# Down product of a SwiGLU layer as seven block products instead of eight, with the sums of activations formed in the gate/up stage

## The chip, the core and the metric

One core of one Trainium2 chip. Its engines run at the same time, each in its own order: TensorE (PE) multiplies a 128x128 block that it has loaded with up to 512 columns, VectorE (DVE) does elementwise work, ScalarE (ACT) copies, squares and activations, GpSimd (POOL) issues some transfers and a power, SyncE (SP) issues most transfers. SBUF is the memory that engines work in, PSUM holds matmul results in 8 banks of 128x512 floats. The metric is device time in microseconds (us) of one execution, lower is better.

## What is computed

A two-layer encoder trunk over 256 + 512 rows of width 1024 (here 768 rows, six tiles of 128). Each layer runs a token mixer and then a SwiGLU, with RMSNorm before and after each. The part that matters is the second:

```python
def swiglu(h, w_gate_up, w_down):          # w_gate_up 1024 x 5632, w_down 2816 x 1024
    g, u = jnp.split(h @ w_gate_up, 2, axis=-1)
    return (jax.nn.silu(g) * u) @ w_down

x = x + rms_norm(swiglu(rms_norm(x, g_pre), ...), g_post)
```

All arrays are float32. The kernel keeps that accuracy by splitting every operand in two fp32r numbers, hi (a rounded copy, made by ACT) and lo (the rest, made by DVE), and by three matmuls for each product: hi·hi, hi·lo, lo·hi.

## The kernel before

**Feed.** `raw_src` lists every weight load in program order and `units` every pair of hi and lo that is made of one, 128x1024 floats at a time. `prepare` makes units up to a ring of five (`RING`, tags `whi`, `wlo`): a unit can be split once TensorE has used the unit five before it. `take` hands units to a product, `free` makes the next ones. Raw weights land in two buffers (`wraw`); `fetch` issues a load on SP as soon as one is free. A planner of the tile library places all instructions in each engine's queue, and every engine, SP too, then runs its queue strictly in order.

**Gate and up** (`ffn`, 22 chunks of 128 hidden units). The activations stand in `h_hi`, `h_lo`; each chunk is already done by seven block products, p1 to p7, of 12 matmuls of 384 columns, over two halves of the hidden width and two halves of the rows (tiles 0 to 2 and 3 to 5). Product p6 puts its result in bank Y (`py`), DVE reads it (`u2`, line 925), and p7 goes on adding into the same bank: between them stands only p2, 12 matmuls. At a chunk's end p3 multiplies by the gate, and POOL stores 384 KB of the chunk's 768 columns to DRAM (`act`, line 953) from a buffer `st`.

**Down** (lines 1007 to 1078). For each half `n2` of the 1024 output columns, 22 chunks are loaded again from DRAM as `araw` (SP, line 1096, two buffers), split to `ahi`, `alo`, and multiplied with the weight units (`down`): a chunk gives 6 tiles x 3 matmuls `pd` of 512 columns, 792 a layer. `Acts.prepare` runs up to six chunks ahead; the first two are loaded before the stage begins, into buffers of the pools `x` and `y` (the second one's `alo` stands in an `x` buffer), since the stage's own pool opens only when the gate/up buffers are gone. `project_end` squares and scales each finished half row; `staged` and `finish` do norms, add the residual `x` (loaded by `load_x` from DRAM into the two `x` buffers), and turn the rows for the next stage.

## Time and profile before

| | |
|---|---|
| runs, us | 1744.67, 1743.99, 1740.69 (median 1743.99) |
| profiled execution, us | 1740.31, of which the span from first to last instruction is 1738.5 |
| mean granted TensorE clock | 0.997 of full speed |
| busy share of the span | PE 98%, DVE 67%, ACT 49%, POOL 5% |
| bytes moved | 187.14 MB, 108 GB/s over the span |

The two gate/up stages lie at about 299 to 629 and 1219 to 1549 us, the down stages at 629 to 813 and 1549 to 1730. A row's `[n <-X]` or `idle before <-X` is the time for which its engine stood still just before it, and what ended that. PE rows overlap: a matmul's row is longer than the distance to the next.

### The profile page before, as it was taken

The numbers are of one execution on the slowest core, as the hardware profiler recorded it, in microseconds if no ns is written. First come the engines' busy times: TensorE is split into PE (matmuls) and PEld (weight loads), VectorE is DVE, ScalarE is ACT, GpSimd is POOL, SyncE is SP. The second block draws the span as 40 slices with busy tenths as digits, with TensorE's granted clock in tenths as the row PEclk, the third lists the DMA queues.
The fourth block names the chain that finished last, engine by engine and source line by source line (L and its number), as shares of the span: only waits on it lengthen the run. The fifth ranks groups of instructions, "written<-read, shape, count | busy, mean of one in ns | idle before, by whom it ended". The sixth has DMA issues, their size and how long they took to land. (4 is left out here: it accounts for less than half of the span.)

```text
span 1738.5 us, 25699 instructions
## 1 busy us (share of the span) xinstructions
PE 1704.5 (98%) x9714; PEld 1552.1 (89%) x9714; DVE 1172.6 (67%) x2368; ACT 854.7 (49%) x1971; POOL 82.3 (5%) x126
## 2 busy tenths in 40 slices
PE   7999999999999999999999999999899999999998
PEld 7888877999999988888999999877899999988886
DVE  7788767887777744446767777757887777744443
ACT  6777766443333333434666666756533333334432
POOL 1000001000000000001000000501000000000000
PEclk9999999999999999999999999999999999999999
DMA  5111105433331266455211111114432322256454
GB/s 206 37 38 46 38 13 196 147 129 99 100 100 64 100 204 197 152 163 179 73 38 37 37 46 39 43 43 162 151 134 100 100 100 76 88 194 197 142 158 139
DMA packets 55484, 187.14 MB, mean 108 GB/s; under 512 B 6720, under 2 KB 7104, under 8 KB 55360
## 3 DMA queue, kind: packets, MB, share of 16 engines
q1 hardware_dynamic: 51696, 167.93, 30.2%
q0 software_dynamic: 3520, 17.30, 2.5%
q8 instruction: 76, 1.25, 0.3%
q14 instruction: 48, 0.39, 0.1%
q10 hardware_dynamic: 144, 0.26, 0.0%
HBM read 155.59 MB, written 29.88 MB: 107 GB/s over the span
## 5 line engine op out<-in xcount | busy, mean ns | idle before, releaser
L202 DVE TENSOR_TENSOR wlo<-wraw,whi 128x1024 fp32r<-128x1024 f32 (+1 forms) x206 | 239.3, 1166 | 118.7 <-ACT whi L201 116.3
L201 ACT CAST whi<-wraw 128x1024 fp32r<-128x1024 f32 (+1 forms) x206 | 204.8, 1001 | 168.6 <-PE px L267 84.4
L266 PE MATMUL pd<-whi,ahi 128*128 128x512 f32 (+1 forms) x550 | 210.7, 383 | 3.8 <-ACT ahi L254 3.8
L267 PE MATMUL pd<-wlo,ahi 128*128 128x512 f32 (+1 forms) x550 | 210.3, 382 | 0.0
L268 PE MATMUL pd<-whi,alo 128*128 128x512 f32 (+1 forms) x550 | 209.1, 381 | 0.0
L255 DVE TENSOR_TENSOR alo<-araw,ahi 128x768 fp32r<-128x768 f32 x88 | 84.0, 958 | 157.5 <-ACT ahi L254 157.4
L254 ACT CAST ahi<-araw 128x768 fp32r<-128x768 f32 x88 | 73.5, 835 | 172.4 <-PE pd L267 94.6
L266 PE MATMUL pqb<-whi,hhi 128*128 128x384 f32 x384 | 136.5, 356 | 0.0
L267 PE MATMUL pqb<-wlo,hhi 128*128 128x384 f32 x384 | 128.9, 336 | 0.0
L268 PE MATMUL pqb<-whi,hlo 128*128 128x384 f32 x384 | 128.8, 335 | 0.0
L266 PEld LDWEIGHTS pd<-whi,ahi 128*128 128x128 f32 x550 | 103.9, 189 | 24.7 <-ACT ahi L254 4.7
L268 PEld LDWEIGHTS pd<-whi,alo 128*128 128x128 f32 x550 | 103.8, 189 | 20.2
L267 PEld LDWEIGHTS pd<-wlo,ahi 128*128 128x128 f32 x550 | 103.7, 189 | 19.5
L266 PE MATMUL px<-hhi,whi 128*128 128x384 f32 x352 | 117.9, 336 | 2.8 <-ACT hhi L254 2.8
L267 PE MATMUL px<-hlo,whi 128*128 128x384 f32 x352 | 117.8, 335 | 2.1 <-DVE hlo L255 2.1
L268 PE MATMUL px<-hhi,wlo 128*128 128x384 f32 x352 | 117.6, 334 | 0.0
L945 ACT ACTIVATE u<-u 128x384 f32<-128x384 f32 x44 | 23.1, 525 | 161.8 <-DVE u L944 161.8
L266 PE MATMUL po<-whi,hhi 128*128 128x512 f32 x192 | 78.0, 406 | 0.2 <-ACT hhi L254 0.2
L268 PE MATMUL po<-whi,hlo 128*128 128x512 f32 x192 | 75.4, 393 | 0.2 <-DVE hlo L255 0.2
L267 PE MATMUL po<-wlo,hhi 128*128 128x512 f32 x192 | 75.3, 392 | 0.0
L266 PEld LDWEIGHTS pqb<-whi,hhi 128*128 128x128 f32 x384 | 72.3, 188 | 1.9 <-issue 1.7
L266 PE MATMUL pqa<-whi,hhi 128*128 128x384 f32 x192 | 73.7, 384 | 0.0
(244 smaller groups left out, 4405.1 us busy)
## 6 DMA issues: line engine op xcount, KB each, us to landing
araw<-act SPq DMA_DIRECT2D x88, 384.0 KB, 3.3
wraw<-in_wgu SPq DMA_DIRECT2D x62, 512.0 KB, 3.5
wraw<-in_wd SPq DMA_DIRECT2D x44, 512.0 KB, 4.1
y_wraw<-in_wgu SPq DMA_DIRECT2D x34, 512.0 KB, 3.5
act<-st POOLq DMA_DIRECT2D x44, 384.0 KB, 2.6
wraw<-in_wb SPq DMA_DIRECT2D x32, 384.0 KB, 3.2
xd<-x SPq DMA_DIRECT2D x18, 512.0 KB, 3.1
x<-xd SPq DMA_DIRECT2D x18, 512.0 KB, 4.1
```

The costliest lines, as they stand in the source:

```text
L201: state["raw_hi"] = nc.scalar.copy(out=hi, in_=src)
L202: state["raw_lo"] = nc.vector.tensor_tensor(out=lo, in0=src, in1=hi.bitcast(F32), op=ALU.subtract)
L254: state["hi"] = nc.scalar.copy(out=hi, in_=src)
L255: state["lo"] = nc.vector.tensor_tensor(out=lo, in0=src, in1=hi.bitcast(F32), op=ALU.subtract)
L266: nc.tensor.matmul(out, ah, bh, start=start and i == 0, stop=False, skip_group_check=more)
L267: nc.tensor.matmul(out, ah, bl, start=False, stop=False, skip_group_check=more)
L268: nc.tensor.matmul(out, al, bh, start=False, stop=stop and i == last, skip_group_check=more)
L945: nc.scalar.activation(out=u, in_=u, func=AF.Silu)
```

## The change

Rows of activations A (two halves of the hidden chunks, two halves of the rows) and the down weights B are cut in 2x2 blocks, and the product is formed by the Winograd form of Strassen's scheme: seven block products, eighteen sums. A half of the hidden width is now every second chunk, so a pair of chunks (2i, 2i+1) holds both halves.

- The sums of activations (`s1` to `s4`, four DVE instructions of 128x384) are made in p3 of every odd chunk, in a buffer `st` of seven parts, and POOL stores all seven (1344 KB a pair). `u2` and `u3` have one buffer instead of two.
- Down runs seven products one after the other, each over 11 pairs in six groups (five of two pairs and one of one). A group is one load of 384 KB of activations, one weight unit and 2 x 3 tiles x 3 matmuls of 512 columns. Products are added up in PSUM where they can be (`V`, `W`); `keep` copies and `add` adds banks into `y`.
- The sums of weights (`t1` to `t4`) are made by DVE in `prepare`, from quarters that are held in the stage's pool (tags `tt`, `rb`) or loaded again into the two `wraw` buffers (t2, b22, t3).
- From the third on, split activations use the slots of `h_hi` and `h_lo`. The finish of tiles 0 to 2 stands inside the sixth product, tiles 3 to 5 end the stage.

```diff
+DOWN = ("b11", "t1", "t2", "b22", "t3", "t4")
+NGRP = (NPAIR + 1) // 2
+RAW = {"w": 2, "y": 2, "tt": 2, "rb": 2}
...
-        for n2 in range(2):
-            for i in range(NPAIR):
-                plain(wd[layer, n2, i], 1024)
+        for kind, quarter, home in (
+                ("plain", (1, 0), "w"), ("b11", (0, 0), "tt"), ("t1", (0, 1), "rb"), ("t2", (1, 1), "w"),
+                ("b22", (1, 1), "w"), ("t3", (1, 0), "w"), ("t4", None, None)):
+            for g in range(NGRP):
...
-            if upto is None and state[home] >= RAW[home]:
+            if upto is None and (state[home] >= RAW[home] or home in quarters and dpool[0] is None):
...
+                if kind in ("t1", "t2"):
+                    nc.vector.tensor_tensor(out=tt, in0=raw, in1=tt, op=ALU.subtract)
+                src = {"b11": raw, "b22": raw, "t3": rb}.get(kind, tt)
...
                 two_parts(hi[:, :n], lo[:, :n], src[:, :n])
+            if kind == "b22":
+                nc.vector.tensor_tensor(out=rb, in0=rb, in1=raw, op=ALU.subtract)
+            elif kind == "t3":
+                nc.vector.tensor_tensor(out=tt, in0=raw, in1=tt, op=ALU.subtract)
...
-            nc.vector.tensor_tensor(out=v[:, :HALF], in0=u, in1=ga.pop(c), op=ALU.mult)
-            nc.gpsimd.dma_start(out=at_hand[c], in_=v)
+            nc.vector.tensor_tensor(out=v[:, 1 - c % 2], in0=u, in1=ga.pop(c), op=ALU.mult)
+            if c % 2:
+                a12, a11, s1, s2, s4, s3, a22 = (v[:, i] for i in range(7))
+                nc.vector.tensor_tensor(out=s1, in0=s3, in1=a22, op=ALU.add)
+                nc.vector.tensor_tensor(out=s2, in0=s1, in1=a11, op=ALU.subtract)
+                nc.vector.tensor_tensor(out=s3, in0=s3, in1=a11, op=ALU.subtract)
+                nc.vector.tensor_tensor(out=s4, in0=a12, in1=s2, op=ALU.subtract)
+                nc.gpsimd.dma_start(out=at_hand[c // 4][:, :, c // 2 % 2], in_=out.pop(c // 2))
...
-                    for c in (2 * i, 2 * i + 1):
-                        for t in range(NT):
-                            down(n2, t, [c], {c: blocks[c % 2]}, c == 0, 0, final and n2 and t == NT - 1)
-                        acts.used(n2, c)
+            def run(p, gs, wk, tiles, into, first=None, last=None, w=512, part=0, more=True):
+                gs = list(gs)
+                todo = [(g, j) for g in gs for j in range(min(2, NPAIR - 2 * g))]
+                for n, (g, j) in enumerate(todo):
+                    a = acts.of(p, g)
+                    b = tuple(v[:, j * 512 + part:j * 512 + part + w] for v in wk[g])
+                    for i in tiles:
+                        products(
+                            into[i][:, :w], [(tuple(v[:, j, i * P:(i + 1) * P] for v in a), b)],
...
+            def begin(t):
+                x_of[t] = load_x(sub, t)
...
+            def add(t, c, b):
+                nc.vector.tensor_tensor(out=y[t][:, c], in0=b, in1=y[t][:, c], op=ALU.add)
+
+            def keep(t, c, b):
+                nc.scalar.copy(out=y[t][:, c], in_=b)
...
+            def one(p, g, into, first=False, last=False):
+                wk = {g: take(1)[0]}
+                run(p, [g], wk, range(3), into, first, last)
+                acts.used(1)
+                free(0)
...
+            whole(0, X, {})
+            V = banks("pv")
+            whole(1, V, {0: [do(keep, i, left, X[i]) for i in range(3)]})
+            X = None
+            W = banks("pw2_")
+            whole(2, W, {i: [do(add, i, left, V[i]), do(half_end, i, left, y[i][:, left], False)] for i in range(3)})
+            whole(3, V, {0: [do(keep, 3 + i, right, W[i]) for i in range(3)]})
+            whole(4, W, {0: [do(keep, i, right, V[i]) for i in range(3)]})
...
+            events = {
+                0: [do(add, i, right, W[i]) for i in range(3)] + [second(0), do(begin, 0), do(stage, 0, 0)],
...
+            for i in range(3):
+                run(5, gs, wk, [i], V, False, True)
+                with tc.high_priority():
+                    add(3 + i, right, V[i])
...
+                    s = self.slot(q)
+                    self.user[s] = q
+                    half, at = divmod(s, 4)
+                    hi, lo = (h[half][:, 2 * at:2 * at + n] for h in (h_hi, h_lo))
```

**SP's queue where the first layer's down stage begins.** `x_0` and `x_1` are the residual rows, `araw` the activations, `act` their DRAM copy, `tt` and `wraw` weights. Before, the two loads of activations stand ahead of `x_1`:

```order
L347 DMA x_0_8243<-xd_0_115 128x1024
L1096 DMA araw_2_7180<-act_2_4249 128x768
L1096 DMA araw_3_7186<-act_3_4250 128x768
L347 DMA x_1_8269<-xd_1_116 128x1024
L196 DMA wraw_7238<-in_wd 128x1024
L1096 DMA araw_4_7192<-act_4_4251 128x768
```

After:

```order
L389 DMA x_0_8056<-xd_0_115 128x1024
L210 DMA wraw_7492<-in_wd 128x1024
L389 DMA x_1_8097<-xd_1_116 128x1024
L1260 DMA araw_2_7181<-act_2_4249 128x768
L1260 DMA araw_3_7185<-act_3_4250 128x768
L210 DMA tt_7205<-in_wd 128x1024
L210 DMA tt_7207<-in_wd 128x1024
L1260 DMA araw_4_7189<-act_4_4251 128x768
```

The load of `x_1` has moved ahead of the third and fourth loads of activations. Its buffer is the one that holds the second activations' `alo`, in both kernels. The second layer has the same order.

**DVE's queue at the end of an odd chunk of gate/up.** `u`, `st`, `py`, `pw`, `ga`, `sv` belong to the chunks, `wraw`, `b`, `wlo` to the weights of later ones. Before, from the silu's factor to the next chunk's read of bank Y:

```order
L946 TENSOR_TENSOR st_13_6081<-st_13_6081,u_13_6062 128x384
L951 TENSOR_TENSOR u_13_6026<-pw_13_6068,u_13_6026 128x384
L202 TENSOR_TENSOR b_6101<-y_wraw_5921,b_6101 128x512
L952 TENSOR_TENSOR st_13_6081<-u_13_6026,ga_13_6040 128x384
L225 TENSOR_TENSOR y_wraw_5921<-y_wraw_5921,wraw_5919 128x512
L226 TENSOR_TENSOR wraw_5919<-y_wraw_5921,wraw_5919 128x512
L202 TENSOR_TENSOR wlo_6100<-y_wraw_5921,whi_6099 128x1024
L925 TENSOR_TENSOR u_14_6153<-py_14_6140,sv_14_6138 128x384
```

After:

```order
L994 TENSOR_TENSOR st_12_5950<-st_12_5950,u_13_6057 128x384
L1003 TENSOR_TENSOR st_12_5950<-st_12_5950 128x384
L999 TENSOR_TENSOR u_13_6021<-pw_13_6063,u_13_6021 128x384
L1004 TENSOR_TENSOR st_12_5950<-st_12_5950 128x384
L216 TENSOR_TENSOR b_6095<-y_wraw_5917,b_6095 128x512
L1000 TENSOR_TENSOR st_12_5950<-u_13_6021,ga_13_6035 128x384
L253 TENSOR_TENSOR y_wraw_5917<-y_wraw_5917,wraw_5915 128x512
L1005 TENSOR_TENSOR st_12_5950<-st_12_5950 128x384
L254 TENSOR_TENSOR wraw_5915<-y_wraw_5917,wraw_5915 128x512
L1006 TENSOR_TENSOR st_12_5950<-st_12_5950 128x384
L216 TENSOR_TENSOR wlo_6094<-y_wraw_5917,whi_6093 128x1024
L968 TENSOR_TENSOR u_14_6151<-py_14_6138,sv_14_6136 128x384
```

The four sums (lines 1003 to 1006) all stand ahead of the read of bank Y (line 968, before 925).

**DVE's queue in the down stage around the end of a set of banks.** Before, at the end of the first half of the columns:

```order
L202 TENSOR_TENSOR wlo_7667<-wraw_7562,whi_7666 128x1024
L510 TENSOR_TENSOR yf_0_7150<-pd_0_0_0_7156,gpost_6883 128x512
L510 TENSOR_TENSOR yf_1_7151<-pd_0_1_0_7160,gpost_6883 128x512
L510 TENSOR_TENSOR yf_2_7152<-pd_0_2_0_7164,gpost_6883 128x512
L510 TENSOR_TENSOR yf_3_7153<-pd_0_3_0_7168,gpost_6883 128x512
```

After, at the end of the fifth product (bank `pw_0_0`):

```order
L264 TENSOR_TENSOR tt_7205<-wraw_7859,tt_7205 128x1024
L264 TENSOR_TENSOR tt_7207<-wraw_7888,tt_7207 128x1024
L216 TENSOR_TENSOR wlo_7916<-rb_7321,whi_7915 128x1024
L264 TENSOR_TENSOR tt_7235<-wraw_7920,tt_7235 128x1024
L216 TENSOR_TENSOR wlo_7941<-rb_7323,whi_7940 128x1024
L264 TENSOR_TENSOR tt_7263<-wraw_7945,tt_7263 128x1024
L264 TENSOR_TENSOR tt_7291<-wraw_7970,tt_7291 128x1024
L216 TENSOR_TENSOR wlo_7966<-rb_7401,whi_7965 128x1024
L264 TENSOR_TENSOR tt_7319<-wraw_7999,tt_7319 128x512
L297 TENSOR_TENSOR hlo_114<-araw_32_7990,hhi_112 128x768
L1106 TENSOR_TENSOR yf_0_7154<-pw_0_0_7512,yf_0_7154 128x512
```

The six sums of the last weights (line 264), each of which reads a newly loaded `wraw`, stand ahead of the first `add` of that bank (line 1106).

## Rows read from the trace of the kernel before

**Rows 1.** The page, busy time: share of the span and instructions.

```profile
PE 1704.5 (98%) x9714; PEld 1552.1 (89%) x9714; DVE 1172.6 (67%) x2368; ACT 854.7 (49%) x1971; POOL 82.3 (5%) x126
```

**Rows 2.** Busy time by stretch: gate/up, then down; x counts instructions.

```profile
470.00:620.00 150.00, 150.00 (x867) 150.00 (x867) 105.57 (x152) 52.98 (x72) 5.96 (x11) 1.00 0.29 99
...
640.00:700.00 60.00, 60.00 (x267) 49.64 (x266) 26.94 (x27) 21.95 (x26) 0.00 (x0) 1.00 0.62 190
```

**Rows 3.** Waits over the span: total us, times, longest us.

```profile
PE pd L266 <- ACT ahi L254: 3.8, 2, 1.9
...
SPq L347 <- PE pd L268: 10.9, 2, 5.4
```

**Rows 4.** Timeline where down begins (PE's first pd at 628.77): SP, ACT, PE.

```profile
630.88 0.83 SPq L1096 DMA_DIRECT2D araw<-act  x2
637.17 0.32 SPq L347 DMA_DIRECT2D x<-xd  x1
...
639.39 0.83 ACT L254 CAST ahi<-araw 128x768 fp32r<-128x768 f32 x1 [0.40 <-DMA araw<-act]
...
639.04 0.50 PE L266 MATMUL pd<-whi,ahi 128*128 128x512 f32 x1 [1.91 <-ACT ahi L254]
```

**Rows 5.** Transfers: KB each, median us to landing; then landing of all araw.

```profile
araw<-act SPq DMA_DIRECT2D x88, 384.0 KB, 3.3
...
wraw<-in_wd SPq DMA_DIRECT2D x44, 512.0 KB, 4.1
...
DMA to landing us min/median/max: 2.8/3.3/8.1
```

**Rows 6.** Stretches after a stall: PE, PEld, DVE, ACT, POOL, granted clock, DMA share, GB/s.

```profile
636.00:640.00 4.00, 2.09 (x10) 1.42 (x9) 1.71 (x2) 2.39 (x3) 0.00 (x0) 1.00 0.85 298
...
1554.00:1558.00 4.00, 2.24 (x6) 1.82 (x7) 2.96 (x3) 2.54 (x3) 0.00 (x0) 0.76 0.74 193
...
1558.00:1562.00 4.00, 4.00 (x16) 3.20 (x15) 0.00 (x0) 0.00 (x0) 0.00 (x0) 0.82 0.82 290
```

**Rows 7.** Groups of one shape: busy us, mean ns of one, idle before.

```profile
L202 DVE TENSOR_TENSOR wlo<-wraw,whi 128x1024 fp32r<-128x1024 f32 x158 | 194.2, 1230 | 110.9 <-ACT whi L201 109.1 <-PE po L268 1.5
L201 ACT CAST whi<-wraw 128x1024 fp32r<-128x1024 f32 x158 | 165.3, 1050 | 153.0 <-PE px L267 84.4 <-PE pd L268 19.2 <-ACT ga L920 16.7
...
L255 DVE TENSOR_TENSOR alo<-araw,ahi 128x768 fp32r<-128x768 f32 x88 | 84.0, 958 | 157.5 <-ACT ahi L254 157.4
...
L254 ACT CAST ahi<-araw 128x768 fp32r<-128x768 f32 x88 | 73.5, 835 | 172.4 <-PE pd L267 94.6 <-DMA araw<-act 73.8 <-DVE wlo L202 2.6
...
L952 DVE TENSOR_TENSOR st<-u,ga 128x384 f32<-128x384 f32 x44 | 24.3, 551 | 0.1
```

**Rows 8.** Timeline of gate/up, DVE then PE: a middle chunk, then chunk 19's end.

```profile
512.49 0.56 DVE L951 TENSOR_TENSOR u<-pw,u 128x384 f32<-128x384 f32 x1 [0.37 <-PE pw L268]
...
513.75 0.55 DVE L952 TENSOR_TENSOR st<-u,ga 128x384 f32<-128x384 f32 x1
514.22 0.69 DVE L225 TENSOR_TENSOR y_wraw<-y_wraw,wraw 128x512 f32<-128x512 f32 x1
...
516.09 1.23 DVE L202 TENSOR_TENSOR wlo<-y_wraw,whi 128x1024 fp32r<-128x1024 f32 x1 [0.45 <-ACT whi L201]
517.23 0.55 DVE L925 TENSOR_TENSOR u<-py,sv 128x384 f32<-128x384 f32 x1
...
518.53 0.33 PE L266 MATMUL py<-hhi,whi 128*128 128x384 f32 x1
...
590.13 0.55 DVE L925 TENSOR_TENSOR u<-py,sv 128x384 f32<-128x384 f32 x1
...
591.33 0.33 PE L266 MATMUL py<-hhi,whi 128*128 128x384 f32 x1
```

**Rows 9.** Timeline of the end: PE's last matmul, DVE's last work.

```profile
1729.94 0.28 PE L268 MATMUL pd<-whi,alo 128*128 128x256 f32 x1
...
1733.77 1.41 DVE L445 SCALAR_TENSOR_TENSOR x<-yf,rstd_last,x 128x512 f32<-128x512 f32 x2 [2.58 <-DMA x<-xd]
```

More of the change, by code (lines that the diff above doesn't have):

```diff
@@ L891, in ffn @@
         sub = 2 * layer + 1
-        at_hand = [dram.tile([P, NT * P], F32, name=f"act{layer}_{c}") for c in range(NCH)]
+        at_hand = [
+            dram.tile([P, 7, min(2, NPAIR - 2 * g), HALF], F32, name=f"act{layer}_{g}") for g in range(NGRP)]
         a_ops = {
@@ new lines, in one, with whole @@
+            def one(p, g, into, first=False, last=False):
[3 more added lines that the diff above has]
+                free(0)
+            def whole(p, into, events):
+                for g in range(NGRP):
+                    one(p, g, into, p in (0, 1, 2) and g == 0, g == NGRP - 1)
+                    for e in events.get(g, ()):
+                        e()
+            do = lambda f, *a: lambda: f(*a)
+            X = banks("px2_")
@@ new lines, in ffn, with last_product @@
+            free(2)
+            V2 = [bank(f"pv2_{k}") for k in range(2)] if final else []
+            def last_product(i, gs, wk, first=False, last=False, parts=(0, 1)):
+                if final and i == 2:
+                    for k in parts:
+                        run(6, gs, wk, [i], {i: V2[k]}, first, last, 256, 256 * k, False)
+                else:
+                    run(6, gs, wk, [i], V, False, last)
+            for i in range(3):
+                last_product(i, gs, wk, True)
+                if i == 0:
+                    stage(2, 2)
+                    begin(3)
+                half_end(3 + i, right, y[3 + i][:, right], False)
@@ new lines, in ffn @@
+            if final:
+                keep(5, left, V[2])
+            acts.used(2)
+            free(0)
+            wk = {2: take(1)[0]}
+            for i in range(3):
+                last_product(i, [2], wk)
+            acts.used(1)
+            free(0)
+            stage(2, 3)
+            begin(4)
+            gs = range(3, NGRP)
+            wk = dict(zip(gs, take(3)))
+            for g in gs:
+                acts.of(6, g)
+            free(3)
+            last_product(0, gs, wk, last=True)
@@ L1082, in trunk @@
+            last_tile(sub, 5, y[5], sq[5], x_of[5], rstd(ss4[:, 1:2], ss[:, 0:1], "last"))
     class Acts:
```

246 lines of the change are left out of this document (152 added, 94 removed).

## The prediction

> **What bounds the kernel now.** I read the busy shares first [rows 1]: TensorE is busy for 98% of the span, DVE for 67%. Then the stretches [rows 2]: 60.00 of 60 us in a down stretch, 150.00 of 150 in gate/up, both at clock 1.00, so in both stages the time is TensorE's work and whatever takes work from it is worth its full time, as long as the others keep up. DVE has room: 105.57 of 150 us in gate/up, 26.94 of 60 in down. Then the waits [rows 3], to see where TensorE stands still already: for `ahi` twice, 3.8 us, once a layer where down begins [rows 4]. The same list shows SP standing at one load until a `pd` matmul is done (10.9 us, twice); the change moves things behind that load.
>
> **What it removes.** A down stage has 22 chunks x 6 tiles x 2 halves x 3 = 792 matmuls. Afterwards it has 7 products x 11 pairs x 3 tiles x 3 = 693 of the same shape: 99 fewer. In the down stretch 267 pass in 60 us [rows 2], 0.2247 us each. 99 x 0.2247 = 22.25 us a layer, **44.5 us** in both, all on the path.
>
> **Where down begins.** Now: `pd` begins at 628.77, two chunks last until 628.77 + 36 x 0.2247 = 636.86, the load of `x_1` goes out at 637.17, when the second chunk's `alo` is used up and its buffer free. The third and fourth activations were asked for at 630.88, ahead of it, and TensorE goes on at 639.04 after 1.91 us [rows 4]. (The cast of the fourth waited for its landing until 639.39.) Afterwards the queue has `x_1` first, and the first two groups last the same 8.09 us, so the third activations are asked for at about 637.6: `x_1` at 637.17, 0.32 to issue, a little between. From there to landing it takes 2.8 us at least, 3.3 in the median, 8.1 at most [rows 5]; 512 KB of `x_1` lie just ahead, and the store of the last pair, 1344 KB in place of 384, goes out some 5 us into the stage and is still under way. The 8.1 was measured at this very place, with a 384 KB store in flight. I take 6.5: landing 644.1, cast 0.83 [rows 7], TensorE on at 644.95, and the third matmul waits some 0.5 us more for `alo`. That is 5.9 + 0.5 = 6.4 us later than 639.04, **12.8 us** for both layers; with 2.8 and 8.1 it is 2.7 and 8.0 a layer.
>
> How the store and the loads share the engines no row tells. The Trainium skill (DMA: Bandwidth & Descriptors, section "Queues, rings and completion order") says that each transfer engine takes turns between queues, packet by packet. By that the 896 KB of `x_1` and the activations run at about half of the 298 GB/s of rows 6 while the store lasts, an estimate of 6.0 us beside the 6.5; wholly behind the store it would be near 8, and the sum 3 us worse.
>
> **The clock.** After the second layer's wait, as long as the first's, the granted clock is 0.76 and 0.82 over two stretches of 4 us: (0.24 + 0.18) x 4 = 1.7 us lost. After the first layer's it stays 1.00 [rows 6]. A wait of 8 us should cost it in both; the second layer pays already: **1.7 us**. Between 0 and another 1.7 for each further stall of 2 us or more.
>
> **Four sums in each odd chunk of gate/up.** One lasts 0.55 us [rows 7], and 0.47 lie between two starts (513.75 and 514.22 [rows 8]): 1.88 us for the four. By the total DVE has the time: 5 pairs in 150 us bring 11, 105.57 becomes 117. But all four stand ahead of the read of bank Y, and p7 adds to that bank. In a middle chunk the read starts at 517.23 and ends at 517.78, p7 begins at 518.53: cover 0.75. Ahead of it DVE stands still for 0.37 (for p3's matmul) and 0.45 (for a cast that itself waits for line 225) [rows 8]. The first takes up most of one sum; the second at most its 0.45, as line 225 is put off as well. 1.88 - 0.37 - 0.45 = 1.06, less the cover 0.75: 0.3 us a pair, for some seven of the eleven. In the last chunks the cover is 591.33 - 590.68 = 0.65 [rows 8], and their loads share with the larger stores: 0.7 each for three. The first four chunks, where DVE is fuller, get 0.7 as well. 7 x 0.3 + 4 x 0.7 = 4.9; as some of it falls into waits that are there already, I take 3.5 a layer, **7 us**. Bounds: 1 (idle time takes all but the last chunks' share) and 8 (no idle time is used and the loads are late: 11 pairs x 0.75).
>
> **Feeding seven products.** A product lasts 99 x 0.2247 = 22.25 us. DVE then has 5.5 weight splits of 1.23, 5.5 activation splits of 0.96 and, for four products, 5.5 sums of the size of a split: 6.8 + 5.3 + 6.8 = 18.9 us [rows 7], 85%. In the products that also empty banks, six more of some 0.7 (the 0.69 of a 512-wide one [rows 8]) make 23.1, over the 22.25. ACT has 5.5 x (1.05 + 0.83) = 10.3 and the bank copies: hidden. The cover for DVE's overrun is the ring: with one unit a group of 4.04 us, a unit may be split four groups, 16 us, before its use. An overrun of 1 us in two products is lost in that. What is not covered by the ring is the `add` that frees a bank: six sums stand ahead of it, each after a new landing in one of two buffers. Per pair of loads 4.1 (landing [rows 5]) + 1.23 + waits, about 6, in the 8.09 us of two groups: it keeps up. I take **2 us** for both layers, from 0 to 8.
>
> At the end, an `add` more in the chain is hidden in the 2.58 us for which the last step waits for `x` [rows 9], whose load stands behind the same store as before: 0, from -1 to 1. Bank copies on ACT, 22 stores in place of 44 on POOL, the finishing of three tiles inside the sixth product: work on engines with room, 0; uncovered they are in the 8 above.
>
> **Sum.** -44.5 + 12.8 + 1.7 + 7 + 2 = -21.0 us. Against the profiled execution: 1740.3 - 21.0 = 1719.3. That execution is 3.7 below the median of the three runs; carried to the median, 1744.0 - 21.0 = **1723 us**.
>
> **Rivals.**
> (a) The covers hold: the late load lands in the median's 3.3 us (3.2 a layer in place of 6.4), gate/up pays 1 a layer. -44.5 + 6.4 + 1.7 + 2 = -34.4: **1710**. For it: most activations land in 2.8 to 3.6. Against: rows 4 and 5, 8.1 at this place.
> (b) DVE falls behind in the middle products and pays at the `add`s: they come 5 us late at the sixth product or at its successor, and the clock dips once more a layer. -21.0 + 2 x (5 + 1.7) = -7.6: **1736**. For it: 85 to 104% of DVE, and each sum waits for ACT or a landing, in order. Against: the ring's 16 us.
> (c) Slower: the reload of weights becomes the bound. t2, b22 and t3 read each weight quarter anew through two buffers; the next load goes out only when the sum has freed one. A pair of loads has 8.09 us; with landing L it takes L + 1.05 + 1.23 and some 0.2, so it decides from L = 5.6. Loads of activations and weights together then ask for 5.5 x 896 KB in 22.25 us, 226 GB/s, where 190 keeps the transfer engines at 0.62 [rows 2]: 0.74. If L goes to the 8.1 of rows 5, a pair takes 10.6, 2.5 too long, 3 pairs x 3 products x 2 layers = 45 us: 1723 + 45 = **1768**.
> (d) It doesn't do what it says. The order has the 693, so only the other terms could hide it: the same as (b).
>
> **How the numbers follow.** Chances: forecast 0.55 (own range 1715 to 1731), (a) 0.15, (b) 0.17, (c) 0.13. The range reaches from (a)'s time to some 6 us beyond (b)'s, 1709 to 1742, and leaves out (c) and a little of (a). 0.2% of the median, about what a measurement of this kernel can tell from no change, is 3.5 us: faster means below 1740.5. The forecast, (a) and most of (b) lie there, 0.81; 0.06 of (b) and of mild forms of (c) lie within; slower is 0.13.
>
> **What would show it.** Right: `pd`'s successors count 693 a layer at 0.2247; the third activations' cast ends TensorE's wait some 16 us after the stage begins; SP's wait for a matmul grows shorter in name but holds both `araw` loads; `py` waits for line 968 in tenths of a us after each odd chunk. Wrong: waits of TensorE for `wlo` in products 3 to 5 (then (c)), or for an `add` or `y_pd` of 3 us and more (then (b)); a first wait below 4 us (then (a)).

## The result, and the profile after

The changed kernel takes 1720.92 us in the median of 4 runs (1719.56 to 1724.5), the kernel before 1743.37 beside it; the ratio is 0.9876, with a 95% interval of 0.9857 to 0.9896. That is 22.4 us less; forecast were 21. The profiled execution has a span of 1718.3 us, against 1738.5.

The page's busy shares, to set beside [rows 1]:

```profile
PE 1666.2 (97%) x9483; PEld 1515.1 (88%) x9483; DVE 1298.3 (76%) x2560; ACT 887.9 (52%) x2026; POOL 83.8 (5%) x104
```

TensorE has 231 instructions less: 198 matmuls of 512 columns, and half of the 66 that the last tile's split into pieces had added (the kernel before has 132 of 256 columns, this one 66). It is busy for 38.3 us less, but the span is only 20.2 shorter, so some 18 us of new standing still lie between. DVE has 126 us more of work, the sums.

The waits over the span, to set beside [rows 3]:

```profile
PE px L308 <- ACT hhi L296: 17.5, 4, 7.5
...
PE py L308 <- DVE u L968: 7.5, 9, 2.1
...
PE pv L308 <- DVE yf L1106: 0.3, 1, 0.3
```

`px` waits for `hhi` where gate/up begins (two short waits that were there before) and where down begins: 7.54 and 7.29 us, in place of 1.91 twice. `py` waits for line 968 nine times; in the kernel before this entry does not exist. The `add` of line 1106, the rival (b), costs 0.3 us. `wlo` does not appear under TensorE: the rival (c) did not come.

The stretches between the first matmuls of the stages, from the timelines of the profiled executions (us; a down stretch ends with the first `pqb`, the second one with the start of the last matmul):

| stretch | before | after | difference |
|---|---|---|---|
| gate/up, layer 0 | 329.76 | 335.97 | +6.2 |
| down, layer 0 | 185.27 | 169.20 | -16.1 |
| gate/up, layer 1 | 329.72 | 336.02 | +6.3 |
| down, layer 1 | 184.46 | 167.32 | -17.1 |
| ahead, between, behind | 709.29 | 709.81 | +0.5 |

**Where down begins.** The timeline of the first layer, SP, POOL, ACT, PE, to set beside [rows 4]:

```profile
641.55 0.33 SPq L210 DMA_DIRECT2D wraw<-in_wd  x1
644.24 0.33 SPq L389 DMA_DIRECT2D x<-xd  x1
644.98 1.41 SPq L1260 DMA_DIRECT2D araw<-act  x2
...
640.59 0.55 POOL L1007 DMA_DIRECT2D act<-st  x1 [27.12 <-DVE st L1006]
...
650.87 1.82 ACT L296 CAST hhi<-araw 128x768 fp32r<-128x768 f32 x2 [10.07 <-DMA araw<-act]
...
651.75 0.79 PE L308 MATMUL px<-whi,hhi 128*128 128x512 f32 x1 [7.54 <-ACT hhi L296]
```

Down begins at 635.85. `x_1` is asked for at 644.24, when the first two groups are through, the third activations at 644.98, and ACT has them at 650.87, 5.9 us later. TensorE goes on 15.9 us after the stage began; the prediction has 16.2. And the clock behind the wait, to set beside [rows 6]:

```profile
642.00:648.00 6.00, 2.21 (x10) 1.50 (x8) 0.00 (x0) 0.00 (x0) 0.00 (x0) 1.00 0.98 346
648.00:654.00 6.00, 2.25 (x5) 1.56 (x6) 1.92 (x2) 2.49 (x3) 0.00 (x0) 0.50 0.95 349
654.00:660.00 6.00, 6.00 (x26) 4.90 (x26) 3.15 (x4) 2.43 (x4) 0.00 (x0) 0.93 0.76 265
```

The granted clock is 0.50 for the 2.25 us in which TensorE worked and 0.93 for the next 6: 1.1 + 0.4 = 1.5 us, now in the first layer too. The transfer engines are at 0.98 and 0.95 all through the wait. What they move from 642 to 646, by queue (q0 is POOL's: 30.28 MB in the whole run, the 22 stores; q1 is SP's, the loads):

```profile
q0 software_dynamic: 123, 1.22, 93.1%
q1 hardware_dynamic: 13, 0.05, 4.5%
```

For these 4 us their time goes to the store, though a load of weights was asked for at 641.55, `x_1` at 644.24 and the activations at 644.98; from 646 to 648 q1 has 99.5%. So what TensorE waits for stands behind the store. In the second layer it is the same (97.7% for q0 and 2.0% for q1 from 1549 to 1553).

**Gate/up.** Three places. The middle chunks, in the weight loads that run ahead of the matmuls:

```profile
433.67 0.19 PEld L308 LDWEIGHTS py<-hhi,whi 128*128 128x128 f32 x1 [0.19 <-DVE u L968]
...
462.94 0.19 PEld L308 LDWEIGHTS py<-hhi,whi 128*128 128x128 f32 x1 [0.19 <-DVE u L968]
```

29.27 us a pair; before, DVE's read of the bank shows 29.12:

```profile
415.31 0.55 DVE L925 TENSOR_TENSOR u<-py,sv 128x384 f32<-128x384 f32 x1
...
444.43 0.55 DVE L925 TENSOR_TENSOR u<-py,sv 128x384 f32<-128x384 f32 x1
```

That is 0.15 a pair, some six pairs. The second chunk, TensorE and then DVE:

```profile
342.79 0.45 PE L308 MATMUL py<-hhi,whi 128*128 128x384 f32 x1 [0.95 <-DVE u L968]
...
341.11 0.55 DVE L1000 TENSOR_TENSOR st<-u,ga 128x384 f32<-128x384 f32 x1
...
342.19 0.55 DVE L968 TENSOR_TENSOR u<-py,sv 128x384 f32<-128x384 f32 x1
```

No sum stands here; the pair is not full yet. But `u2` has one buffer where the kernel before has two, and line 968 writes it: it has to follow line 1000, which reads it for the chunk before. In the kernel before, the same read starts 2.75 us ahead of that product:

```profile
337.26 0.55 DVE L925 TENSOR_TENSOR u<-py,sv 128x384 f32<-128x384 f32 x1
...
340.01 0.55 DVE L952 TENSOR_TENSOR st<-u,ga 128x384 f32<-128x384 f32 x1
```

And the timeline of the twentieth chunk, SP, POOL, DVE, PE:

```profile
580.19 0.33 SPq L210 DMA_DIRECT2D wraw<-in_wgu  x1
...
582.67 0.33 SPq L210 DMA_DIRECT2D wraw<-in_wgu  x1
...
580.92 0.90 POOL L1007 DMA_DIRECT2D act<-st  x1 [30.32 <-DVE st L1006]
...
589.67 0.69 DVE L251 TENSOR_TENSOR wraw<-wraw,wraw 128x512 f32<-128x512 f32 x1 [3.23 <-DMA wraw<-in_wgu]
...
597.76 0.44 PE L308 MATMUL py<-hhi,whi 128*128 128x384 f32 x1 [2.12 <-DVE u L968]
```

The stretches there:

```profile
580.00:584.00 4.00, 3.68 (x21) 3.36 (x20) 2.78 (x5) 1.78 (x3) 0.90 (x1) 1.00 0.65 222
584.00:588.00 4.00, 4.00 (x25) 4.00 (x24) 1.79 (x3) 0.71 (x1) 0.00 (x0) 1.00 1.00 304
```

The chunk's two loads of weights are asked for at 580.19 and 582.67, the 1344 KB store at 580.92 between them; the engines are full (1.00) from 584 to 588, and from 583 to 586 q0, the store, has 97.4% of their time and q1, the loads, 1.8%. DVE waits 3.23 us for the weights, all that stands behind on its queue is late, and TensorE waits 2.12 us, eight us further on. No sum lies between. In the second layer the same wait is 1.93 us.

Where the 6.2 and 6.3 us of the two gate/up stretches are lost can be read from the starts of p7's first matmul in each chunk, before and after: 1.3 and 2.5 us up to the second chunk, 1.4 and 1.1 from there to the eighteenth, 3.4 and 2.9 in the nineteenth to twenty-first. The clock of the first 31 us is no part of it in the first layer: 0.96 before, 0.95 after.

### The profile page after: what moved, and what is told of

It is laid out like the page before. It is cut to its first block, busy times and chain, and to the rows that moved or that the text cites. A ratio compares the mean times of both kernels' runs of the same rounds, so it can differ in the third digit from the quotient of the medians.

```text
span 1718.3 us, 25415 instructions
## 1 busy us (share of the span) xinstructions
PE 1666.2 (97%) x9483; PEld 1515.1 (88%) x9483; DVE 1298.3 (76%) x2560; ACT 887.9 (52%) x2026; POOL 83.8 (5%) x104
## 3 DMA queue, kind: packets, MB, share of 16 engines
q1 hardware_dynamic: 55152, 175.15, 30.7%
q0 software_dynamic: 6688, 30.28, 5.4%
## 5 line engine op out<-in xcount | busy, mean ns | idle before, releaser
L216 DVE TENSOR_TENSOR wlo<-wraw,whi 128x1024 fp32r<-128x1024 f32 (+2 forms) x186 | 212.5, 1148 | 89.4 <-ACT whi L215 88.6
L215 ACT CAST whi<-wraw 128x1024 fp32r<-128x1024 f32 (+2 forms) x186 | 182.4, 987 | 180.7 <-PE px L309 70.8
L296 ACT CAST hhi<-araw 128x768 fp32r<-128x768 f32 (+1 forms) x74 | 57.5, 782 | 98.2 <-DMA araw<-act 84.1
L297 DVE TENSOR_TENSOR hlo<-araw,hhi 128x768 fp32r<-128x768 f32 (+1 forms) x74 | 65.4, 890 | 44.5 <-ACT hhi L296 43.7
L308 PE MATMUL pv<-whi,hhi 128*128 128x512 f32 (+1 forms) x240 | 92.4, 385 | 0.3 <-DVE yf L1106 0.3
L310 PE MATMUL pv<-whi,hlo 128*128 128x512 f32 (+1 forms) x240 | 92.1, 384 | 0.0
L309 PE MATMUL pv<-wlo,hhi 128*128 128x512 f32 (+1 forms) x240 | 92.1, 384 | 0.0
L309 PEld LDWEIGHTS pqb<-wlo,hhi 128*128 128x128 f32 x384 | 72.4, 188 | 0.6 <-DVE wlo L216 0.5
L310 PEld LDWEIGHTS pqb<-whi,hlo 128*128 128x128 f32 x384 | 72.1, 188 | 0.0
L308 PEld LDWEIGHTS px<-hhi,whi 128*128 128x128 f32 x352 | 65.9, 188 | 3.8 <-ACT hhi L296 3.2
```

The lines of the kernel that those rows point to most:

```text
L215: state["raw_hi"] = nc.scalar.copy(out=hi, in_=src)
L216: state["raw_lo"] = nc.vector.tensor_tensor(out=lo, in0=src, in1=hi.bitcast(F32), op=ALU.subtract)
L296: state["hi"] = nc.scalar.copy(out=hi, in_=src)
L297: state["lo"] = nc.vector.tensor_tensor(out=lo, in0=src, in1=hi.bitcast(F32), op=ALU.subtract)
L308: nc.tensor.matmul(out, ah, bh, start=start and i == 0, stop=False, skip_group_check=more)
L309: nc.tensor.matmul(out, ah, bl, start=False, stop=False, skip_group_check=more)
```

## The experiments

Each kernel is the changed one with an edit, if nothing else is said; each was timed against the kernel before in the same session, whose medians were 1741.66 to 1742.65. The chunk that the expectations call the twenty-first is the twentieth.

**x_later.** The loads of `x_0` and `x_1` no longer stand ahead of the third and fourth activations.

```diff
             def begin(t):
-                x_of[t] = load_x(sub, t)
+                with tc.issue_after(acts.load[3].ins):
+                    x_of[t] = load_x(sub, t)
...
-                nc.sync.dma_start(out=raw, in_=self.at[g][:, p])
+                self.load[q] = nc.sync.dma_start(out=raw, in_=self.at[g][:, p])
```

> The changed kernel, with the loads of the residual rows x_0 and x_1 of each down stage put behind the third and fourth loads of activations on SP's queue (they come to stand behind the fourteenth); nothing else. Theory A (the third activations are late because x_1 stands ahead of them and waits for TensorE): they are asked for about 2 us after the stage begins, TensorE's first wait in down falls from 7.5 and 7.3 us to 1 to 3, and the clock dip behind it gets smaller; 5 us a layer and 0 to 3 of clock, 10 to 13 us off 1721: 1708 to 1711. Theory B (the 1344 KB store, which goes out 4.7 us into the stage, holds them up whatever the order): the loads are asked for earlier but land with the store all the same; the wait stays at 5 us or more and at most 4 us are won: 1717 to 1721.

Measured: 1722.7 us, ratio 0.9887 (0.9872 to 0.9903): nothing won. The timeline of this kernel, SP, ACT, PE, and then its stretches:

```profile
640.44 2.37 SPq L1261 DMA_DIRECT2D araw<-act  x2
...
647.48 0.83 ACT L296 CAST hhi<-araw 128x768 fp32r<-128x768 f32 x1 [8.25 <-DMA araw<-act]
...
648.37 0.79 PE L308 MATMUL px<-whi,hhi 128*128 128x512 f32 x1 [5.72 <-ACT hhi L296]
```

```profile
646.00:650.00 4.00, 1.64 (x4) 1.05 (x5) 1.26 (x2) 1.67 (x2) 0.00 (x0) 0.54 1.03 414
650.00:654.00 4.00, 4.00 (x13) 3.17 (x12) 1.88 (x2) 1.81 (x2) 0.00 (x0) 0.61 0.80 234
```

The stage begins at 634.29. The activations are asked for 6.2 us into it, 3 us sooner than in the changed kernel (9.1), but not at 2: another load, of `wd`, stands ahead of them and waits until the weight unit before it is split, which needs the ring slot that the first group of `px` gives back. And they take 7.0 us to come: from 640 to 644 the store has all of the engines' time and SP's queue none,

```profile
q0 software_dynamic: 127, 1.37, 100.0%
```

The wait shrinks by 1.8 and 1.7 us only, the low clock behind it lasts longer (0.46 x 1.64 + 0.39 x 4 = 2.3 us against 1.5), and in the second layer 2.92 us of waiting for an `add` come up, which stands on DVE behind a step that waits 2.84 us for a row of `x` (in the changed kernel that step waits 1.88 and the `add` costs 0.25). Theory A in its pure form is wrong: the order of `x_1` is a part of the delay of the request, not its cause alone.

**small_store** and **x_later_small_store.** Two of the seven blocks are stored; in the second with the edit of x_later.

```diff
-                nc.gpsimd.dma_start(out=at_hand[c // 4][:, :, c // 2 % 2], in_=out.pop(c // 2))
+                nc.gpsimd.dma_start(out=at_hand[c // 4][:, 3:5, c // 2 % 2], in_=out.pop(c // 2)[:, 3:5])
...
-                nc.sync.dma_start(out=raw, in_=self.at[g][:, p])
+                nc.sync.dma_start(out=raw, in_=self.at[g][:, 3 + p % 2])
```

> The changed kernel with stores of 384 KB a pair of chunks in place of 1344: two of the seven blocks are stored, and every load of activations reads one of these two, so that the down product is not the reference's; sizes, counts and order of all loads stay. Theory A (the store shares the transfer engines with the loads that TensorE waits for): the activations at the start of down land in 3 to 4 us in place of 5.9, the wait falls from 7.5 to about 5, and the wait of 2.1 us at the twenty-first chunk of gate/up goes: 4 to 5 us a layer, 8 to 10 off 1721, 1711 to 1713. Theory B (only the order of SP's queue and of DVE matters): both waits stay within 0.5 us, 1719 to 1721.

> The edits of x_later and of small_store together (two of seven blocks stored, so that the product is not the reference's). First wait in the first down stage so far: 7.5 as changed, 5.7 with x later, 3.9 with the small store. Theory A (order and shared transfer engines each hold a part, and what is left is another load of weights that stands ahead in the queue until TensorE has used up a weight): asked for 6.2 us into the stage, landing in 3.5, cast 0.83, cover 8.1: a wait of 2 to 2.5. Theory B (the one is the other seen twice): 3.5 to 3.9 as with the small store alone.

Measured: 1714.44 us (0.985, 0.9828 to 0.9871) and 1714.19 (0.9835, 0.9813 to 0.9857). The timeline of small_store, SP, ACT, PE:

```profile
638.77 1.36 SPq L1260 DMA_DIRECT2D araw<-act  x2
...
644.00 0.83 ACT L296 CAST hhi<-araw 128x768 fp32r<-128x768 f32 x1 [6.43 <-DMA araw<-act]
...
644.89 0.79 PE L308 MATMUL px<-whi,hhi 128*128 128x512 f32 x1 [3.89 <-ACT hhi L296]
```

The first expectation did not hold in one point: with the smaller store the scheduler itself put `x_1` behind the activations. So in the order that counts both runs are x_later (`x_0` stays ahead in small_store), and they agree: asked for 6.1 us into the stage, wait 3.89 and 3.82. The second run's expectation of 2 to 2.5 fell, since it was made from another order. What the three runs do give is the store's share at one and the same order: from asking to the cast 7.0 us with 1344 KB, 5.2 with 384; 1.8 to 1.9 us of waiting in the first layer, 2.5 to 2.6 in the second. And the wait at the twentieth chunk is gone from both profiles, in small_store with DVE's wait for the weights (0.19 in place of 3.23). So that wait is the store's, and of the first wait of down a part: most of the 5.2 us that are left is the loads among themselves (from 640 to 644 q1 has 93.2% of the engines in small_store), and the kernel before, too, had 8.1 us here beside 384 KB. Every load of these two runs reads one of the same two blocks; that this alone changes nothing was not tested. Against x_later the time is 8 us less, by the ratios 6 and 9.

But in these profiles the down stretches are hardly shorter than the changed kernel's 169.20 and 167.32: 169.31 and 166.89 in small_store, 167.21 and 166.55 in the other. What its shorter first wait won (3.65 and 4.23 us), small_store lost again behind it. In the first layer the clock was low for longer: 0.50 over 3.11 us of TensorE's work and 0.65 over the next 4, 3.0 us in place of 1.5; 1.48 us of waiting for `y_pd` and 0.58 for an `add` came up. In the second the `add` cost 3.70 in place of 0.25. The gain in time is gate/up's, 2.3 and 2.2 us.

**early_acts.** The third and fourth activations are loaded in gate/up's last chunk but one, into buffers of `sv` and `ga` that are free by then.

```diff
             p3(c)
+            if c == NCH - 2:
+                acts.early(cpool)
+        acts.prepare(4)
         steps.close()
...
+        def early(self, pool):
+            for q, tag in ((2, "sv"), (3, "ga")):
+                bufs = AHEAD + 1
+                self.pre[q] = [
+                    pool.tile([P, HALF], F32, tag=tag, name=f"araw{self.layer}_{q}_{j}", bufs=bufs) for j in range(2)]
+                for j in range(2):
+                    nc.sync.dma_start(out=self.pre[q][j], in_=self.at[q][:, 0, j])
```

> The changed kernel, with the third and fourth loads of activations of each down stage put into free buffers of gate/up (four tiles of 128x384) and asked for while gate/up still runs, in its last chunk but one; all else stays, x_1 ahead of the fifth and sixth loads too. Theory A (TensorE's first wait in down is the time from asking to landing of these two loads, whether the order of the queue or the 1344 KB store stretches it): the wait of 7.5 and 7.3 us goes, and the clock dip behind it; 7 + 1.5 us a layer, less up to 2 for the fifth and sixth: 13 to 17 us off 1721, 1704 to 1708. Theory B (the queue and the store hold up the next loads just as much): the wait moves to the fifth activations, 4 us or more stay, 1712 to 1717.

Measured: 1711.84 us, ratio 0.9826 (0.9813 to 0.984): 9 us off: the wait goes, as theory A has it, but the time is the 1712 of theory B. Stretches of the first down stage (PE, PEld, DVE, ACT, POOL, clock, DMA share, GB/s):

```profile
636.00:642.00 6.00, 6.00 (x29) 5.10 (x28) 5.43 (x10) 0.90 (x2) 0.45 (x1) 1.00 0.58 165
642.00:648.00 6.00, 6.00 (x29) 4.95 (x28) 0.52 (x1) 0.00 (x0) 0.10 (x1) 1.00 0.93 323
```

The wait is gone and with it the low clock; the fifth activations, asked for 8.8 us into the stage behind `x_1`, are not missed. The two down stretches are 164.37 and 159.10 us, 13.1 less together. The rest of the expectation did not come: later in down 2.72 us of waiting for `y_pd` and 1.35 for an `add` stand in the profile, and its gate/up stretches are 2.1 and 1.5 us longer, at a granted clock of 0.89 in their first 31 us (layer 0) against 0.95 in the profile of after, and with waits of 0.48 and 0.65 at the twenty-first chunk that the changed kernel does not have.

**sums_later** and **both_later.** The four sums and the store stand behind the next chunk's read of bank Y; in the second run with the edit of x_later.

```diff
-            if c % 2:
+            if c == NCH - 1:
+                sums(c)
+        def sums(c):        # s1 to s4 and the store, as in p3
...
+            read = nc.vector.tensor_tensor(out=u2[c], in0=Y[c], in1=sv[c], op=ALU.add)
+            if c and c % 2 == 0:
+                with tc.issue_after(read.ins):
+                    sums(c - 1)
```

> The changed kernel, with the four sums of an odd chunk of gate/up (and their store) put behind the next chunk's read of bank Y on DVE; those of the last chunk stay. Theory A (TensorE waits in gate/up because the sums stand ahead of that read): the gaps of 0.2 to 0.5 us at each odd chunk's end and the longer waits at the early and late chunks go, 6.2 us a layer, 12 us off 1721: about 1709. Theory B (only the gaps of the middle chunks are the order's; the 2.1 us wait of a late chunk comes from a weight load that shares the transfer engines with the 1344 KB store, and DVE is simply full in the first four chunks): the middle gaps go, 2.2 us a layer, and a part of the rest; 5 to 7 us off: 1714 to 1716.

> Both edits, the x loads behind the activations and the sums behind the next read of bank Y. If the two terms are independent, the savings add: by the two theories A 1721 - 12 - 12 = 1697, by the two theories B about 1711 to 1715. If the store of the last pair, which stays where it was, holds the activations up, the sum is missed in the down stage's first wait alone.

Measured: 1717.48 us (0.9862, 0.9842 to 0.9882) and 1715.74 (0.9848, 0.9827 to 0.9869). A pair of middle chunks takes 29.12 us again, as before the change; the waits at the second and the twentieth chunk stay:

```profile
342.91 0.45 PE L308 MATMUL py<-hhi,whi 128*128 128x384 f32 x1 [0.94 <-DVE u L968]
...
595.57 0.44 PE L308 MATMUL py<-hhi,whi 128*128 128x384 f32 x1 [2.20 <-DVE u L968]
```

By the rows that is theory B: the sums' place on DVE costs the middle gaps and the third chunk's 0.46, not more. The times alone can't tell it, since the intervals of both runs overlap the changed kernel's (0.9857 to 0.9896).

**sums_at_c22.** The same, further back: the sums follow the addition that reads bank W (`c22`) in the next chunk.

```diff
+            read = nc.vector.tensor_tensor(out=out[c // 2][:, 5 + c % 2], in0=W[c], in1=u3[c], op=ALU.add)
+            if c and c % 2 == 0:
+                with tc.issue_after(read.ins):
+                    sums(c - 1)
```

> The changed kernel with the four sums of an odd chunk and their store put further back than in the run sums_later: behind the addition that reads bank W in the next chunk. Where DVE then stood idle for some 3 us, and the weights of the late chunks have landed when the store goes out. Theory A (the 2.1 us at the twenty-first chunk is the store's collision with its two weight loads): that wait goes too, besides the middle gaps (0.15 us a pair) and the 0.46 of the third chunk: 3.5 us a layer, 1713 to 1715. Theory B (the wait comes from that chunk's loads alone, or the store hits the next loads in their turn): as sums_later, 1717.

Measured: 1716.16 us, ratio 0.9853 (0.9833 to 0.9873), between the two expectations, and its interval too overlaps the changed kernel's; the rows decide. The timeline, POOL, then TensorE's wait and DVE's queue ahead of it, and the stretch in which the first of the stores goes out:

```profile
584.79 0.91 POOL L1014 DMA_DIRECT2D act<-st  x1 [28.03 <-DVE st L1013]
614.05 0.91 POOL L1014 DMA_DIRECT2D act<-st  x1 [28.36 <-DVE st L1013]
...
623.29 0.44 PE L308 MATMUL py<-hhi,whi 128*128 128x384 f32 x1 [2.12 <-DVE u L968]
...
621.81 0.96 DVE L297 TENSOR_TENSOR alo<-araw,ahi 128x768 fp32r<-128x768 f32 x1 [4.93 <-ACT ahi L296]
622.69 0.55 DVE L968 TENSOR_TENSOR u<-py,sv 128x384 f32<-128x384 f32 x1
```

```profile
582.00:586.00 4.00, 4.00 (x25) 4.00 (x24) 3.92 (x9) 0.72 (x2) 0.91 (x1) 1.00 0.09 35
```

The store goes out at 584.79, when the transfer engines are idle (0.09) and the twentieth chunk's weights have come, and that chunk's wait is gone from the profile: together with small_store, where the store is smaller and stays in its place, that shows the collision from two sides. But the next store, at 614.05, now goes out 0.9 us ahead of the load of the first activations (614.96), whose split stands ahead of the last chunk's read of bank Y: 2.12 us there, and 1.24 in the second layer. The wait has moved with the store.

**two_u2.** Two buffers for `u2`; `sv` has four in place of five.

```diff
-            sv[c] = temp("sv", c, AHEAD + 1, cpool)
+            sv[c] = temp("sv", c, AHEAD, cpool)
-            u2[c] = temp("u2", c, 1)
+            u2[c] = temp("u2", c, 2)
```

> The changed kernel with two buffers in place of one for u2, the sum that reads bank Y (as the kernel before has it; the tile sv gives up one of its five buffers for the room). Theory A (at the second chunk of gate/up the read of bank Y can't start before the first chunk's u2 is used up, since there is only one): the wait of 0.95 us at the second chunk goes in both layers, the rest stays; some 2 us off 1721: about 1719, too little for the comparison to tell, so the row of that wait decides. Theory B (DVE is merely full there): the wait stays.

Measured: 1723.49 us, ratio 0.9887 (0.9868 to 0.9905): no gain. The row of the second chunk's wait is gone in both layers, so its cause was the buffer; but

```profile
343.63 0.44 PE L308 MATMUL pz<-hhi,whi 128*128 128x384 f32 x1 [0.38 <-ACT whi L215]
...
353.32 0.44 PE L308 MATMUL py<-hhi,whi 128*128 128x384 f32 x1 [1.10 <-DVE u L968]
```

0.38 us for a weight cast (a row that the kernel before has too, 0.37) and 1.10 in place of 0.46 at the third chunk, where the sums stand ahead of the read, take its place. So one buffer and the sums' place hide each other: giving back the buffer pays only where the sums have moved as well (in combined the row of 1.10 is gone).

**gate_up_alone.** The kernel before, with `c22`, `c21`, `p3`, the store and the single buffers of the changed one, and its own down stage.

```diff
-            nc.gpsimd.dma_start(out=at_hand[c], in_=v)
+            if c % 2:
+                ...                                   # the four sums
+                nc.gpsimd.dma_start(out=at_hand[c // 4][:, :, c // 2 % 2], in_=out.pop(c // 2))
...
-                nc.sync.dma_start(out=raw, in_=self.at[q % NCH])
+                src = self.at[c // 4]                 # c = q % NCH
+                src = src[:, c % 4] if c < 20 else src[:, 2 * (c % 2):2 * (c % 2) + 2, 0]
+                nc.sync.dma_start(out=raw.rearrange("p (a b) -> p a b", a=2), in_=src)
```

> The kernel before with the gate/up stage of the changed one alone: the four sums in each odd chunk and one store of 1344 KB a pair of chunks; the down stage keeps its eight blocks, 792 matmuls a layer and the order of its loads (it reads the new layout in pieces of the same size, so that it multiplies other blocks than it should). By the trace of the changed kernel gate/up is 6.2 us a layer longer: 12.5 us over 1743, and 0 to 4 more where down begins, since the last store is now 1344 KB: 1756 to 1760. By the prediction's own sizes 7 us: 1750. If gate/up's loss hung on the seven products' weights being loaded (which the kernel before does not do), it would be under 5: below 1748.

Measured: 1768.34 us, ratio 1.0145 (1.0129 to 1.0161), 26.5 us slower than the kernel before, above all three expectations. Its waits:

```profile
PE pd L266 <- ACT ahi L254: 13.4, 2, 7.0
...
PE py L266 <- DVE u L927: 7.6, 9, 2.3
```

The gate/up stretches are 8.6 and 8.4 us longer than before, in the first layer with the changed kernel's waits at the same chunks (0.95, 0.43, 1.94); where down begins, 7.0 and 6.3 us in place of 1.9 twice. In this kernel too the scheduler put `x_0` and `x_1` ahead of the third activations, which are asked for 8.8 us into the stage, though its down code is the old one; so the run does not tell order from store. What it does tell: the whole loss of the change, the first wait of down included, comes with gate/up's half (the sums, their store, their buffers, and the order that the scheduler makes of it), and the seven products take next to nothing of their own: from this kernel to the changed one the down stretches shrink from 192.10 and 189.18 us to 169.20 and 167.32, 44.8 in all, where the matmuls are 44.5.

**combined**, **combined_split**, **combined_store.** Early activations, sums at `c22`, x later (behind the sixth load of activations), two buffers for `u2`. Then, each alone on top of it: the splits of the first two activations behind the last chunk's read of bank Y; and the last store but one back in its own chunk.

```diff
 combined_store, against combined:
-            if c == NCH - 1:
+            if c >= NCH - 3 and c % 2:
                 sums(c)
...
-            if c and c % 2 == 0:
+            if c % 2 == 0 and 0 < c < NCH - 2:
```

> Four edits: the third and fourth loads of activations early (as early_acts), the sums and stores as in sums_at_c22, the x loads behind the activations, and two buffers in place of one for the sum of bank Y that the second chunk has to wait for (the silu's factor gives up one of five buffers for it). By the sums of the parts: 13 to 17 + 6 to 7 + 2 (0.95 us a layer at the second chunk, by that wait's row) off 1721: 1695 to 1700. If the parts overlap (the store that is later in gate/up meets the early loads), 1702 or more.

> The run combined, with the splits of the first two activations of each down stage put behind the last chunk's read of bank Y on DVE; their loads stay. In combined that read stood behind the first split, whose load took 6.6 us beside the 1344 KB store, and TensorE waited 2.75 and 2.64 us for it. If that is so, the waits go: 5 us and up to 2 of clock off 1702: 1696 to 1698. If the late split holds up the next read of DVE in its place (the one that frees bank W), 1700 to 1702.

> The run combined, with the sums and the store of the last pair but one put back to the end of their own chunk, so that the store goes out some 5 us before the load of the first activations and not 1 us. If the collision of this store with that load is what TensorE waits for (2.75 and 2.64 us), the wait falls under 0.5 us, and the gap that the sums cost at that chunk's end (0.3) comes back: 4 to 5 us off 1702, 1697 to 1698. If the store's 4.5 us of transfer still reach into the load, half of that.

Measured: 1702.27 (0.9779, 0.9764 to 0.9793), 1701.56 (0.9761, 0.9743 to 0.9778) and 1696.82 us (0.9737, 0.9722 to 0.9751). In combined the wait has moved as in sums_at_c22, in order DVE and PE:

```profile
623.38 0.96 DVE L297 TENSOR_TENSOR alo<-araw,ahi 128x768 fp32r<-128x768 f32 x1 [5.70 <-ACT ahi L296]
...
624.85 0.44 PE L308 MATMUL py<-hhi,whi 128*128 128x384 f32 x1 [2.75 <-DVE u L968]
```

Both cures remove it. With the splits put back, gate/up is 329.95 us in the first layer, as long as before the change, but the profile shows other waits in down, 2.30 us for `y_pd` and 3.25 for an `add` behind a late row of `x`, and the time stays. With the store put back it is 0.20 us there (timeline, PE), and the first 24 us of down have no gap (one of four stretches):

```profile
623.28 0.44 PE L308 MATMUL py<-hhi,whi 128*128 128x384 f32 x1 [0.20 <-DVE u L968]
```

```profile
638.00:644.00 6.00, 6.00 (x29) 4.95 (x28) 0.00 (x0) 0.00 (x0) 0.00 (x0) 1.00 0.97 349
```

The transfer engines are as full (0.97) as in the changed kernel at this place; the store still goes out. Only what it delays has been asked for early enough. This is the best version: 46 us below the kernel before and some 24 below the changed one. Against the kernel before, its down stretches are 50.8 us shorter, the 44.5 of the matmuls and more, since the 1.9 us of waiting at each start of down and the low clock behind one of them are gone as well; its gate/up stretches are still 6.1 us longer.

## Why the prediction was right, point by point

**The sum was right by a cancellation.** Forecast -21.0, measured -22.4 by the medians and -20.2 by the profiled spans. The down stages came out better (-33.2 against -44.5 + 12.8 + 1.7 + 2 = -28.0), gate/up worse (+12.5 against +7). Of the 5 us in down the terms below explain about half: with the sizes measured they make -44.5 + 12 + 1.5 + 0.3 = -30.7. For the other 2.5 us no row was found.

**What it removes, 44.5.** Right. The matmuls are 693 a layer at 0.2247; in combined_store the down stretches are 160.44 and 158.52 us, shorter than before by 24.8 and 25.9, which is 22.25, the 1.9 us of waiting and, in the second layer, the 1.7 of clock that stood at the start (24.2 and 25.9).

**Where down begins, 12.8.** Right in the time, half right in the cause. Asked for 8.8 us into the stage by the prediction, 9.1 measured; 6.5 us to land, 5.9 measured; on at 16.2, 15.9 measured; 5.6 and 5.4 us a layer and about 0.5 for `alo` (1.0 us over two waits in the weight loads) are 12 us. But the prediction reads as if `x_1` were the cause. x_later took it out of the way and won nothing: the load of weights behind it holds the queue until 6.2 us, and the loads then stand behind the store. The runs at one order put the larger store at 1.8 to 2.6 us of the wait; the 6.5 us were taken between the median and the 8.1 of the place, not from a mechanism.

The prediction set beside this term what the Trainium skill (DMA: Bandwidth & Descriptors, section "Queues, rings and completion order") says of engines that take turns between queues, packet by packet. It made of that half the rate for the loads while the store lasts, and 6.0 us; the trace has 5.9. The number fits and the working does not: from 642 to 646 the store had 93.1% of the engines and the loads 4.5%, in x_later 100.0% and nothing. That is the other case that it named, wholly behind the store, which it put near 8; it came out shorter because the store was through by 646, at 1.22 MB in 4 us, and the loads had the engines to themselves after it. So 5.9 against 6.0 is luck. How much of a store counts as one packet no run here shows.

**The clock, 1.7.** Right: 1.5 us in the first layer, and in the second 1.8 (0.50 over 1.79 us of work, 0.78 over the next 4), as much as the 1.7 before.

**Gate/up, 7.** The step that failed. It was one term, four sums ahead of one read, and the measured 12.5 us are three. The term itself was too large in the middle: 0.15 us a pair, not 0.3. (Its count is off too: three late pairs and the two of the first four chunks are five of the eleven, and six are left, not four and seven.) What made up for it, and more, it did not have. The 2 us at the twentieth chunk were bounded as "their loads share with the larger stores: 0.7 each for three", a cover taken from the read's place on DVE; but a late load stops DVE's whole queue, 3.23 us, and then only the chunk's slack counts. And the diff's second buffer of `u2` and `u3`, taken away for room, was read and not costed: 0.95 us a layer at the second chunk, though two_u2 did not get it back alone. By stretches, the middle cost 1.4 and 1.1 us (worked out at 2.1), the late chunks 3.4 and 2.9 (at 2.1). The bounds, 2 to 16 for both layers, hold the 12.5.

**Feeding, 2; the end, 0.** 0.3 us at one `add`; the stretch behind the last matmul is 7.4 us in place of 8.6, a little over the bound of 1.

**Rivals.** (a), 1710, had its condition refuted: the first wait is 7.5 us, not below 4. (b) and (c) did not come; DVE falls behind nowhere in the middle products. That the place of (b) is tender is shown by x_later, early_acts, combined_split and both runs with the small store, where 1.4 to 3.7 us of waiting for an `add` appear in the second layer, each time behind a step that waits 1.5 to 2.8 us for a row of `x`, and not for DVE's load as (b) had it. What gate/up loses up to the second chunk lies between 0.2 and 4.5 us over the profiles of all runs, so the changed kernel's 1.3 and 2.5 us there are the least certain of the 12.5.

## What to carry to other kernels

A larger store is not free because it runs on an idle queue: look for the loads that are asked for within a few us of it and for who waits for them, and move either the store by some us or the request ahead of it. When a wait has two causes in a row (a queue's order, then a slow landing), undoing one shows little; asking earlier takes away both. A wait that only gets shorter may win nothing: the clock behind it and the next late load can take it back, so compare the length of the stage and not the row of the wait. A buffer that a change takes away for room is a cost like an added instruction: find the write that must now follow the last read, and what else holds the same place.

## What the runs showed of the hardware that was not expected

The granted clock after a wait of 7.5 us with TensorE idle was 0.50 over 2.25 us of work and 0.93 over the next 6; after a shorter wait, 5.7 us in x_later, it was 0.54 and 0.61 over 5.6 us of work. The shorter wait cost more clock: 2.3 us against 1.5. So of the 1.8 us that the order won there, 0.8 went back; in the second layer it is 2.9 against 1.8 (0.58 over 2.60 us of work and 0.56 over the next 4), 1.1 of 1.7, and small_store's 3.89 us cost 3.0. The clock was low before TensorE came back (0.50 from 648 on in the changed kernel, where it came back at 651.75), and the sooner it came back the more of its work met the low clock.

The first 31 us of gate/up, whose matmuls the edits hardly touch, ran at granted clocks between 0.89 (early_acts, sums_at_c22) and 1.00 (combined, x_later) in single profiles, up to 3.4 us of difference. A stage's length from one profile is worth no more than that.

With a 1344 KB store and several loads asked for, the engines' time went to the store for 3 to 4 us, and the loads got 0 to 5% of it (four places above); with the 384 KB store at the twentieth chunk of small_store, from 580 to 583, the two had 28.1% and 56.1%.

The transfer engines moved 414 GB/s over 4 us in x_later when the store was through and loads of activations and of weights were under way, and 304 to 349 in the stretches where TensorE and DVE waited: a stretch is full by the busy share, not at one rate.
